# Spreading the mixer's loads over slots and sharing the second projection's weights between both halves, in a fused decoder layer

## The chip, the cores and the metric

One core of one Trainium2 chip runs the whole layer in one launch. The core has a matmul engine (TensorE, PE in the profile, with its weight loads listed as PEld), a vector engine (VectorE, DVE), a scalar engine (ScalarE, ACT), GpSimd (POOL), and SyncE (SP), whose queue issues almost all DMA transfers. SBUF is the on-chip memory, PSUM the banks that matmuls write, and DRAM lies off the core. The metric is the device time of one launch in microseconds, lower is better; shown are the median and the spread of several runs.

## The reference

One decoder layer on a sequence of 1024 tokens with a model width of 1024, in float32, with 256 memory tokens:

```python
h = rmsnorm(x, ln1)
ml_qk, ml_v, ml_o, ml_i, ml_f, fx_q, fx_k, fx_v, fx_f = split(h @ w_in)
ml_out = mlstm_chunkwise(...)            # 4 heads of width 128, normalised and gated
fx_out = forgetting_attention(...)       # 8 heads of width 64, causal
x = x + concatenate([ml_out, fx_out], -1) @ w_out          # 1024 x 1024
x = x + cross_attention(rmsnorm(x, ln_x), rmsnorm(mem, ln_mem), w_xq, w_xkv, w_xo)  # 4 heads of 256
u = relu(rmsnorm(x, ln2) @ w_ff1)        # 1024 x 4096
x = x + (u * u) @ w_ff2
out = rmsnorm(x, ln_f)
```

The change concerns the product with w_out, which joins the two groups of heads and adds the result to x, and the keys and values of the cross attention that are computed beside it.

## The kernel before

Activations lie with the model dimension on the 128 partitions, in 8 blocks (`KT`), and with the tokens in the free dimension, in two halves of 512 (`TH`, `hf`). A float32 factor is kept as two parts, hi (rounded to fp32r) and lo (the rest): `split` makes hi on ACT (line 130) and lo on DVE (line 131). A product is then three matmuls, lo by hi, hi by lo and hi by hi (`mm3`, lines 182 to 184), each of 512 columns. Weights come as raw tiles `wr`, in two buffers, and are cut into `wh` and `wl`.

**The mixer's result.** The four mLSTM heads and the attention's heads write their hi and lo parts to a DRAM tensor `mix[hf, part, partition, k]`. Its block index k runs over 8 blocks: 0 to 3 are the mLSTM heads, 4 the attention's heads 0 and 1, 5 heads 2 and 3, 6 heads 4 and 5, 7 heads 6 and 7. The product with w_out is done in two passes. The first uses k = 0 to 4 (`w_out_a`), runs while the attention is still going on, and writes x plus its partial sum to DRAM as `x1d`. The second uses k = 5 to 7 (`w_out_b`) and runs after the attention; it reads `x1d`, adds, and writes the sum back for later use.

**The attention's slots.** The attention runs as a list of slots (`slot`). In each, every engine gets a little of several steps at different stages: transposes of probabilities on PE (line 767, to PSUM bank `tp`), their cut into hi and lo, products with the values (line 786, to `ov`), scores of a later tile (lines 719 and 720, to `sc`), maxima on DVE, exponentials on ACT (line 741), scaling on POOL. `in_order` keeps the order of each engine as it is written, SP's among them in most slots; each engine works its queue in that order. One DMA of the next head's queries and keys is issued in each slot while there are any (`fx_step`, line 701, tensor `fqk`).

**The filler.** PE's time that the attention leaves in a slot is filled from a second list, `units`: 12 units that compute the cross attention's keys and values (`key_unit`, `value_unit`, results stored to `kxd` and `vxd`), and then 16 units of the first pass (`out_unit(hf, n)`, one for each half and output block n). A unit yields step by step to its slot. Its weights are cut by half tiles (line 965 on ACT, and DVE and POOL in turn for lo), and the raw load of the next ones is issued one slot after a cut (`raw_load`, line 952). `mix_in(0)` loads what half 0 needs of mix: two transfers of 1 MB into a tile `act` (line 850, k = 0 to 3, hi and lo) and two of 256 KB into a tile `z` (line 856, k = 4). It stands ten units into the list; `mix_in(1)` does the same for half 1 at `out_unit(0, 4)`. The residual tile of x comes with the unit that adds it (line 925, added at line 933). It and the results of the keys and values turn round in three buffers, `rotate("p", "a")`: two of tag p, one of tag a.

**The second pass.** After the slots, `mix_load` brings k = 5 to 7 of half 0, 768 KB for each part, and `out_proj` goes through the 8 output blocks of half 0 and then of half 1. A weight tile of 128x768 holds three k-blocks for two output blocks n; it is loaded and cut for each half anew, so eight times. `full_sink` adds `x1d`, stores the sum, splits it into `h2` for the cross attention, and has POOL add its squares to an accumulator (`acc`, DVE's tiles r_e among the squares). `row_second(hf, acc)` makes the normalising factors of one half: `rsqrt_sums` sums the squares with four small matmuls and takes the power on POOL, `to_row` turns them into a row by a transpose and a round trip through DRAM. It runs for half 0 at n = 2 of half 1, and for half 1 after the cross attention's first head of the first half. The cross attention follows, then the MLP.

```python
units += [out_unit(hf, n) for hf in range(2) for n in range(KT)]
...
fx_step()
part = next(parts, None)
...
todo_ = late[:]        # work that an earlier slot put off to this one
```

Of the kernel before, what the change touches and what calls it, by code (L numbers as in the profile page):

```python
# [17 lines left out]
P = 128  # L18
T = 1024
# [25 lines left out]
def hybrid_layer(ctx: ExitStack, tc: tile.TileContext, a: dict, out: bass.AP):  # L45
# [750 lines left out]
        v.tensor_tensor(out=om[hf][rng], in0=ov[0:FXD], in1=t[0:FXD], op=ALU.add)  # L796

    def fx_store(hd, hf):
        hi, lo = w2("y", dt=F32R), om[hf].bitcast(F32R)
        split(hi, lo, om[hf])  # L800

        def store():
            load(mix[hf, 0, :, MLH + hd // 2], hi.bitcast(F32))
            load(mix[hf, 1, :, MLH + hd // 2], lo.bitcast(F32))

        late.append(store)
# [37 lines left out]

    x1d = dram.tile([2, P, KT, TH], F32, name="x1d")

    def mix_load(k0, k1, hf):
        t = act().rearrange("p (e k) c -> p e k c", e=2)
        for p_ in range(2):
            load(t[:, p_, : k1 - k0].bitcast(F32), mix[hf, p_, :, k0:k1])  # L850
        return [(t[:, 0, k], t[:, 1, k]) for k in range(k1 - k0)]

    def mix_tile(k, hf):
        t = z4()[:, :T].bitcast(F32R).rearrange("p (e c) -> p e c", e=2)
        for p_ in range(2):
            load(t[:, p_].bitcast(F32), mix[hf, p_, :, k])
        return t[:, 0], t[:, 1]

    def out_proj(w_src, src, hf, sink):

        kn = len(src)
        per = w_src.shape[2] // (kn * P)
        for n in range(KT):
            if n % per == 0:
                w = both(weights(w_src[n // per], kn * per * P), lambda t: t.rearrange("p (k c) -> p k c", k=kn))
            at_ = n % per * P
            ps = mm()
            for k in range(kn):
                mm3(ps, both(w, lambda t: t[:, k, at_ : at_ + P]), src[k], k == 0, k == kn - 1)
            sink(n, hf, ps)  # L870


    late = []

    def void(_):
        return None

    def key_unit(n):
        def run(ws):
            w = both(ws[0], lambda t: t.rearrange("p (k c) -> p k c", k=KT))  # L880
            ps = mm()
            for k in range(KT):
# [12 lines left out]

        return [a["w_xk"][n]], run

    def value_unit(hd):
        def run(ws):
            ws = [both(w, lambda t: t.rearrange("p (k c) -> p k c", k=4)) for w in ws]  # L900
            for t in range(2):
                ps = mm()[:, :NM]
                for k in range(KT):
                    x = (hm[:, 0, k, t * P : (t + 1) * P], hm[:, 1, k, t * P : (t + 1) * P])
                    mm3(ps, x, both(ws[k // 4], lambda z: z[:, k % 4]), k == 0, k == KT - 1)
                    yield 1.5, k == KT - 1, lambda: sink(t, ps)

        def sink(t, ps):
            o = rotate("p", "a").bitcast(F32R).rearrange("p (e c) -> p e c", e=2)
# [5 lines left out]
    mixes = {}  # L915

    def mix_in(hf):
        mixes[hf] = mix_load(0, MLH, hf) + [mix_tile(k, hf) for k in range(MLH, MLH + KX)]

    def out_unit(hf, n):  # L920
        def run(ws):
            if n == 4 and hf == 0:
                mix_in(1)
            x = rotate("p", "a")
            load(x, a["x"][:, n, hf * TH : hf * TH + TH])
# [75 lines left out]
    def slot(values, until):  # L1001
        with in_order((*COMPUTE, mybir.EngineType.SP) if values or until else COMPUTE):
# [83 lines left out]
    while late:  # L1086
        late.extend(filter(None, [late.pop(0)()]))
    banks[:] = ["mm", "tp", "m2", "tp"]
    mix_fx = [mix_load(MLH + KX, KT, 0)]
    h2 = []  # L1090
    mix_done = []
    for hf in range(2):
        hi, lo = act(), act()
        acc = w2("b")

        def full_sink(n, hf, ps):
            t = rotate("p", "d", "e")
            with tc.issue_after(last_raw[0].ins):
                load(t, x1d[hf, :, n])
            v.tensor_tensor(out=t, in0=ps, in1=t, op=ALU.add)  # L1100
            done = load(x1d[hf, :, n], t)
            if hf == 0 and n == 1:
                with tc.issue_after(done.ins):
                    mix_fx.append(mix_load(MLH + KX, KT, 1))
            split(hi[:, n], lo[:, n], t, vec[:, VEC["ln_x"] + n :][:, 0:1])
            square_sum(acc, t, n == 0, add=g)
            if hf == 1 and n == KT - 3:
                mix_done.append(done)
            if hf and n == 2:
                row_second(0, acc0)  # L1110

        def row_second(hf, acc):
            c = rcol[:, 4 * hf : 4 * hf + 4]
            rsqrt_sums(acc, c, 4)
            at = slice(hf * TH, hf * TH + TH)
            to_row(row[:, at], c, 4, rowd[2:3, at])

        out_proj(a["w_out_b"], mix_fx[hf], hf, full_sink)
        h2.append((hi, lo))
        acc0 = acc  # L1120


    def cross_head(hd, hf, oh, ol):
# [174 lines left out]
    for hf in range(2):  # L1298
        oh, ol = act(), act()
        for hd in range(XH):  # L1300
# [5 lines left out]
            for _ in steps:  # L1306
                pass
            if hd == hf == 0:
                row_second(1, acc0)
        os_.append((oh, ol))  # L1310
    for n in range(2, KT):
        first_half(n)
# [362 lines left out]
```

## Time and profile before

| | |
|---|---|
| runs | 1532.7, 1533.2, 1538.22 us; median 1533.2 |
| profiled execution | 1537.44 us, of which the span of all engines' work is 1535.7 |
| mean granted clock of PE | 0.996 of full speed |
| busy | PE 1504.1, PEld 1260.2, DVE 1102.0, ACT 731.7, POOL 505.4 us |
| DMA | 303.53 MB moved, 198 GB/s over the span |
| attention with filler, up to the second pass | ends at about 610 us |
| second pass | about 610 to 656 us |

How to read the views that follow. In the timeline a row has the start in us, the duration, the engine, the line of the kernel, the operation with what it writes and reads (buffer numbers left out), and in brackets how long the engine had been idle before it and what ended that. "SPq" is SP's queue issuing a transfer, so its row gives when the transfer was handed over, not when the data came. The view of waits has for each waiting group and its releaser the sum, the number and the longest of the waits. The table of stretches has for each stretch of the span its length, then the busy time and the number of instructions of PE, PEld, DVE, ACT and POOL, the granted clock, the mean busy share of the DMA engines, and GB/s.

### The profile page before, as it was taken

The page shows a single profiled execution, that of the slowest core. Times are in us where ns is not written, and L with a number is a line of the kernel's source. Part 1 is how long each engine was busy: PE and PEld are TensorE (multiplying, and loading weights), DVE is VectorE, ACT ScalarE, POOL GpSimd, SP SyncE. Part 2 cuts the span into 40 slices and gives each one's busy share as a digit, 9 for nine tenths or more (in the row PEclk, how much of TensorE's full clock was granted, in tenths as well). Part 3 has the DMA queues.
Part 4 walks back from the last instruction along what each step waited for, and adds up shares of the span by engine and source line. Part 5 has one row for each costly group of instructions (what it writes and reads, how often), then busy time and mean ns, then how long its engine had stood idle before and what let it go on. Part 6 is the DMA issues. An engine that isn't in the chain of part 4 may idle for free. (4 is left out here: it accounts for less than half of the span.)

```text
span 1535.7 us, 21948 instructions
## 1 busy us (share of the span) xinstructions
PE 1504.1 (98%) x7665; PEld 1260.2 (82%) x7665; DVE 1102.0 (72%) x1747; ACT 731.7 (48%) x1365; POOL 505.4 (33%) x543
## 2 busy tenths in 40 slices
PE   8999999999999999999999999999999999999997
PEld 8878888889998878788888877787787888888887
DVE  7656676764787776944557889888887567887665
ACT  7324343334686665644444457666665621121224
POOL 1002030413364442521110023554454365563322
PEclk9999999999999999999999999999999999999999
DMA  6422223435889786963344428777667777776623
GB/s 221 124 76 76 96 104 117 134 128 155 245 243 262 228 262 205 349 211 118 124 131 162 167 90 296 245 250 243 227 246 273 303 288 270 275 271 238 246 96 110
DMA packets 121530, 303.53 MB, mean 198 GB/s; under 512 B 13502, under 2 KB 28152, under 8 KB 113996
## 3 DMA queue, kind: packets, MB, share of 16 engines
q1 hardware_dynamic: 121420, 302.13, 58.2%
q8 instruction: 60, 0.98, 0.3%
q14 instruction: 50, 0.41, 0.1%
HBM read 202.22 MB, written 99.86 MB: 197 GB/s over the span
## 5 line engine op out<-in xcount | busy, mean ns | idle before, releaser
L182 PE MATMUL tp<-act,wl 128*128 128x512 f32 (+1 forms) x448 | 176.2, 393 | 1.8 <-DMA act<-mix 0.8
L183 PE MATMUL tp<-act,wh 128*128 128x512 f32 (+1 forms) x448 | 175.4, 391 | 0.0
L184 PE MATMUL tp<-act,wh 128*128 128x512 f32 (+1 forms) x448 | 175.0, 392 | 0.0
L131 DVE TENSOR_TENSOR wl<-wr,wh 128x1024 fp32r<-128x1024 f32 (+2 forms) x99 | 129.7, 1310 | 20.8 <-ACT wh L130 19.9
L130 ACT ACTIVATE wh<-wr 128x1024 fp32r<-128x1024 f32 (+2 forms) x99 | 98.9, 1000 | 84.0 <-PE tp L184 36.5
L182 PE MATMUL mm<-act,wl 128*128 128x512 f32 (+1 forms) x336 | 129.8, 386 | 0.9 <-DVE r_c L514 0.9
L183 PE MATMUL mm<-act,wh 128*128 128x512 f32 (+1 forms) x336 | 129.2, 385 | 0.0
L184 PE MATMUL mm<-act,wh 128*128 128x512 f32 (+1 forms) x336 | 128.9, 383 | 0.0
L182 PE MATMUL m<-act,wl 128*128 128x512 f32 (+1 forms) x312 | 119.7, 384 | 3.1 <-DVE wl L131 2.1
L184 PE MATMUL m<-act,wh 128*128 128x512 f32 (+1 forms) x312 | 119.7, 384 | 0.0
L183 PE MATMUL m<-act,wh 128*128 128x512 f32 (+1 forms) x312 | 119.3, 382 | 0.0
L182 PEld LDWEIGHTS tp<-act,wl 128*128 128x128 f32 x448 | 84.2, 188 | 21.7 <-ACT row L1368 1.2
L184 PEld LDWEIGHTS tp<-act,wh 128*128 128x128 f32 x448 | 84.2, 188 | 19.2
L183 PEld LDWEIGHTS tp<-act,wh 128*128 128x128 f32 x448 | 84.2, 188 | 18.9
L182 PE MATMUL sc<-act,wl 128*128 128x512 f32 (+1 forms) x248 | 97.0, 391 | 0.9 <-DVE wl L131 0.8
L183 PE MATMUL sc<-act,wh 128*128 128x512 f32 (+1 forms) x248 | 96.7, 390 | 0.0
L184 PE MATMUL sc<-act,wh 128*128 128x512 f32 (+1 forms) x248 | 96.7, 390 | 0.0
L130 ACT ACTIVATE wh<-z 128x1024 fp32r<-128x1024 f32 (+1 forms) x54 | 55.5, 1027 | 82.6 <-POOL z L1439 60.9
L1439 POOL TENSOR_TENSOR z<-wr 128x256 f32<-128x256 f32 x56 | 50.4, 921 | 133.7 <-DMA wr<-w_ff2q 126.3
L131 DVE TENSOR_TENSOR wl<-z,wh 128x1024 fp32r<-128x1024 f32 (+1 forms) x54 | 74.8, 1385 | 9.8 <-ACT wh L130 9.7
L130 ACT ACTIVATE w<-wr 128x768 fp32r<-128x768 f32 (+2 forms) x31 | 25.5, 824 | 105.0 <-PE tp L182 32.8
L182 PEld LDWEIGHTS mm<-act,wl 128*128 128x128 f32 x336 | 63.4, 189 | 13.8 <-DVE r_c L514 1.2
(683 smaller groups left out, 4254.8 us busy)
## 6 DMA issues: line engine op xcount, KB each, us to landing
act<-right SPq DMA_DIRECT2D x49, 1024.0 KB
right<-w SPq DMA_DIRECT2D x56, 256.0 KB
wr<-w_ff2q SPq DMA_DIRECT2D x28, 512.0 KB
right<-r_d SPq DMA_DIRECT2D x49, 256.0 KB
right<-r_e SPq DMA_DIRECT2D x49, 256.0 KB
act<-fqk SPq DMA_DIRECT2D x48, 256.0 KB
wr<-w_in SPq DMA_DIRECT2D x20, 512.0 KB
wr<-w_ff SPq DMA_DIRECT2D x20, 512.0 KB
```

The costliest lines, as they stand in the source:

```text
L130: s.activation(hi, src, AF.Copy)
L131: return v.tensor_tensor(out=lo, in0=src, in1=hi.bitcast(F32), op=ALU.subtract)
L182: nc.tensor.matmul(ps, w[1], x[0], start=first, stop=False, skip_group_check=more)
L183: nc.tensor.matmul(ps, w[0], x[1], start=False, stop=False, skip_group_check=more)
L184: nc.tensor.matmul(ps, w[0], x[0], start=False, stop=last, skip_group_check=more)
L1439: g.tensor_tensor(out=o, in0=x, in1=y, op=op)
```

## The change

**Loads of mix in pieces.** `mix_in(hf)` only allocates its tiles, and puts ten copies of 256 KB (one for each k and part) on a list `pieces`. `mix_step`, called once in each slot behind `fx_step`, issues the first of them. `mix_in(0)` stands one unit earlier than before. What is left of the list when a half's first unit starts is issued there at once. SP's queue from the first mix load to the first weights of the first pass, before (raw weight buffers are `wr`, "x2" means two such rows):

```order
L952 DMA wr_5096<-w_xk 128x1024
L701 DMA act_3178<-fqk 64x1024
L850 DMA act_5122<-mix 128x2048 x2
L856 DMA z_886_5125<-mix 128x512 x2
L701 DMA act_3178<-fqk 64x1024
L829 DMA w_896_5159<-fvd 128x1024
L701 DMA act_3178<-fqk 64x1024
L892 DMA kxd<-r_p_5120 256x1x256
L952 DMA wr_5182<-w_out_a 128x640
```

and the same place of the changed kernel, from the second piece on (a first one stands two rows ahead):

```order
L919 DMA act_5021<-mix 128x512
L874 DMA kxd<-r_b_5017 256x1x256
L960 DMA wr_5100<-w_xk 128x1024
L701 DMA act_3178<-fqk 64x1024
L919 DMA act_5021<-mix 128x512
L701 DMA act_3178<-fqk 64x1024
L919 DMA act_5021<-mix 128x512
L834 DMA w_896_5159<-fvd 128x1024
L701 DMA act_3178<-fqk 64x1024
L919 DMA act_5021<-mix 128x512
L874 DMA kxd<-r_p_5125 256x1x256
L960 DMA wr_5183<-w_out_a 128x640
```

Two pieces stand ahead of the last w_xk, three between it and the first w_out_a, and five behind that.

**Residual tiles one unit ahead.** `x_in` loads the residual tile of the next unit, not of the unit that runs, and the tiles of units turn round in five buffers, `ROOM = ("p", "b", "p", "b", "a")`, not three. SP's queue where half 1's mix loads begin, before and after:

```order
L952 DMA wr_5755<-w_out_a 128x640
L850 DMA act_5801<-mix 128x2048 x2
L856 DMA z_1046_5804<-mix 128x512 x2
L925 DMA r_p_5807<-x 128x512
L701 DMA act_3178<-fqk 64x1024
L934 DMA x1d<-r_a_5699 128x512
L701 DMA act_3178<-fqk 64x1024
L952 DMA wr_5876<-w_out_a 128x640
```

Now, from the same load of w_out_a on:

```order
L960 DMA wr_5763<-w_out_a 128x640
L923 DMA r_b_5811<-x 128x512
L701 DMA act_3178<-fqk 64x1024
L919 DMA act_5809<-mix 128x512
L942 DMA x1d<-r_a_5614 128x512
L701 DMA act_3178<-fqk 64x1024
L919 DMA act_5809<-mix 128x512
L960 DMA wr_5882<-w_out_a 128x640
L701 DMA act_3178<-fqk 64x1024
L919 DMA act_5809<-mix 128x512
L923 DMA r_p_5905<-x 128x512
```

The residual tile r_b_5811 is that of the following unit, and the mix pieces stand behind it, one for each slot.

**The last two heads' results stay on chip.** `fx_store` puts the hi and lo parts of heads 6 and 7 into a tile of tag w4 for each half, not into mix. `mix_fx_in`, at the start of head 7's values, puts eight pieces (k = 5 and 6 of both halves) on the list, into one tile `act`. So `mix_load`, `mix_tile` and `out_proj` go.

**The second pass in chunks of four.** For output blocks 0 to 3 and then 4 to 7, two weight tiles are loaded and cut, and used for half 0 and then for half 1: four loads and cuts, not eight. Factors of half 0 are summed after block 6 of half 1, those of half 1 where they were, and one `to_row` then writes the row for both. PE's queue at the start of the second pass, before (tp, m and mm are PSUM banks, ov that of the attention's values):

```order
L786 MATMUL ov_6593<-r_d_6713,w_1173_6297 128x256
L182 MATMUL tp_6792<-act_6763,wl_6772 128x512
L786 MATMUL ov_6593<-w_1269_6724,w_1173_6297 128x256 x2
L182 MATMUL m_1271_6732<-act_5801,wl_6616 128x512
L183 MATMUL m_1271_6732<-act_5801,wh_6615 128x512
L184 MATMUL m_1271_6732<-act_5801,wh_6615 128x512
L182 MATMUL m_1271_6732<-z_1046_5804,wl_6616 128x512
```

and now, with w_1256 the kept result of heads 6 and 7 of half 0:

```order
L786 MATMUL ov_6612<-r_d_6734,w_1174_6311 128x256
L182 MATMUL tp_6813<-act_6528,wl_6787 128x512
L183 MATMUL tp_6813<-act_6528,wh_6786 128x512
L184 MATMUL tp_6813<-act_6528,wh_6786 128x512
L182 MATMUL tp_6813<-act_6528,wl_6787 128x512
L183 MATMUL tp_6813<-act_6528,wh_6786 128x512
L184 MATMUL tp_6813<-act_6528,wh_6786 128x512
L182 MATMUL tp_6813<-w_1256_6669,wl_6787 128x512
L183 MATMUL tp_6813<-w_1256_6669,wh_6786 128x512
```

The second pass's first block stands whole ahead of the attention's last products, which followed its first matmul before. The sums of half 0 (`row_second(0)`) now stand among the first matmuls of the cross attention's queries.

The diff, cut to its core:

```diff
     def fx_store(hd, hf):
+        if hd == FXH - 1:
+            t = w4(dt=F32R)
+            mix_fx[hf].append((t[:, :TH], t[:, TH:]))
+            split(*mix_fx[hf][-1], om[hf])
+            return
...
+            if hd == FXH - 1:
+                mix_fx_in()
...
+    ROOM = ("p", "b", "p", "b", "a")
...
-            t = rotate("p", "a").rearrange("p (e c) -> p e c", e=2)
+            t = rotate(*ROOM).rearrange("p (e c) -> p e c", e=2)
...
     def mix_in(hf):
-        mixes[hf] = mix_load(0, MLH, hf) + [mix_tile(k, hf) for k in range(MLH, MLH + KX)]
+        t = act().rearrange("p (e k) c -> p e k c", e=2)
+        mixes[hf] = [(t[:, 0, k], t[:, 1, k]) for k in range(MLH)]
...
+        pieces.extend((mixes[hf][k][p_], mix[hf, p_, :, k]) for k in range(MLH + KX) for p_ in range(2))
...
+    def mix_step():
+        if pieces:
+            dst, src = pieces.pop(0)
+            load(dst.bitcast(F32), src)
...
     def out_unit(hf, n):
         def run(ws):
+            while n == 0 and pieces:
+                mix_step()
             if n == 4 and hf == 0:
                 mix_in(1)
-            x = rotate("p", "a")
-            load(x, a["x"][:, n, hf * TH : hf * TH + TH])
+            if hf == 0 or n + 1 < KT:
+                x_in(hf + (n + 1) // KT, (n + 1) % KT)
+            x = xs.pop((hf, n))
...
-            if u == len(units) - 2 * KT - 2:
+            if u == len(units) - 2 * KT - 3:
                 mix_in(0)
+            if u == len(units) - 2 * KT - 1:
+                x_in(0, 0)
...
             fx_step()
+            mix_step()
...
+    for n0 in (0, 4):
+        ws = [weights(a["w_out_b"][n0 // 2 + i], 6 * P) for i in range(2)]
+        for hf in range(2):
...
+            for n in range(n0, n0 + 4):
...
+                full_sink(n, hf, ps)
+                if hf and n == 6:
+                    row_second(0)
```

More of the change, by code (lines that the diff above doesn't have):

```diff
@@ L845, in hybrid_layer @@
     x1d = dram.tile([2, P, KT, TH], F32, name="x1d")
[L847 to L870, printed above, removed]
     late = []
+    ROOM = ("p", "b", "p", "b", "a")
     def void(_):
@@ L908, in sink @@
         def sink(t, ps):
-            o = rotate("p", "a").bitcast(F32R).rearrange("p (e c) -> p e c", e=2)
+            o = rotate(*ROOM).bitcast(F32R).rearrange("p (e c) -> p e c", e=2)
             split(o[:, 0], o[:, 1], ps, rcol_m[:, t : t + 1])
@@ L1088, in hybrid_layer @@
     banks[:] = ["mm", "tp", "m2", "tp"]
-    mix_fx = [mix_load(MLH + KX, KT, 0)]
-    h2 = []
+    h2 = [(act(), act())]
+    x1_accs = [w2("b"), w2("b")]
     mix_done = []
[L1092 to L1120, printed above, removed]
@@ new lines, in full_sink, with row_second @@
+    def full_sink(n, hf, ps):
+        hi, lo = h2[hf]
+        t = rotate("p", "d", "e")
+        with tc.issue_after(last_raw[0].ins):
+            load(t, x1d[hf, :, n])
+        v.tensor_tensor(out=t, in0=ps, in1=t, op=ALU.add)
+        done = load(x1d[hf, :, n], t)
+        split(hi[:, n], lo[:, n], t, vec[:, VEC["ln_x"] + n :][:, 0:1])
+        square_sum(x1_accs[hf], t, n == 0, add=g)
+        if hf == 1 and n == KT - 3:
+            mix_done.append(done)
+    def row_second(hf):
+        rsqrt_sums(x1_accs[hf], rcol[:, 4 * hf : 4 * hf + 4], 4)
+        if hf:
+            to_row(row, rcol, 8, rowd[2:3])
@@ new lines, in hybrid_layer @@
+    for n0 in (0, 4):
+        ws = [weights(a["w_out_b"][n0 // 2 + i], 6 * P) for i in range(2)]
+        for hf in range(2):
+            if len(h2) <= hf:
+                h2.append((act(), act()))
+            for n in range(n0, n0 + 4):
+                w = both(ws[n // 2 % 2], lambda t: t.rearrange("p (k c) -> p k c", k=3)[:, :, n % 2 * P : n % 2 * P + P])
+                ps = mm()
+                for k in range(3):
+                    mm3(ps, both(w, lambda t: t[:, k]), mix_fx[hf][k], k == 0, k == 2)
+                full_sink(n, hf, ps)
+                if hf and n == 6:
+                    row_second(0)
@@ L1308, in hybrid_layer @@
             if hd == hf == 0:
-                row_second(1, acc0)
+                row_second(1)
         os_.append((oh, ol))
```

13 lines of the change are left out of this document (12 added, 1 removed).

## The prediction

> **What bounds the kernel now.** I read the page first, then the waits of the matmul engine, then the timeline around its longest waits, then a table by stretches.
>
> ```profile
> span 1535.7 us, 21948 instructions
> PE 1504.1 (98%) x7665; PEld 1260.2 (82%) x7665; DVE 1102.0 (72%) x1747; ACT 731.7 (48%) x1365; POOL 505.4 (33%) x543
> ```
>
> The matmul engine (PE) is busy for 98% of the span. Nearly every microsecond of the kernel is a matmul that the change keeps, so it can only win the time in which PE stands still or runs slowly. The stages that the change touches run from about 475 to 660 us. PE's waits of over half a microsecond there, from the view of waits:
>
> ```profile
> PE sc L719 <- ACT act L741: 4.6, 3, 3.2
> ...
> PE tp L767 <- DVE r_e L131: 1.1, 2, 0.9
> PE m L182 <- DVE r_e L1100: 1.0, 1, 1.0
> ...
> PE tp L182 <- DMA act<-mix: 0.8, 1, 0.8
> ```
>
> The columns are the sum, the number and the longest. The largest is a single wait of 3.2 us for the exponentials on ACT. The timeline tells what ACT had been doing:
>
> ```profile
> 498.70 0.47 ACT L965 ACTIVATE wh<-wr 128x320 fp32r<-128x320 f32 x1 [5.16 <-DMA wr<-w_out_a]
> ...
> 500.17 0.80 PE L719 MATMUL sc<-act 128*128 128x512 f32 x1 [3.23 <-ACT act L741]
> ...
> 504.60 0.63 PE L182 MATMUL mm<-act,wl 128*128 128x512 f32 x1
> 505.03 0.63 PE L183 MATMUL mm<-act,wh 128*128 128x512 f32 x1
> ...
> 506.22 0.39 PE L183 MATMUL mm<-act,wh 128*128 128x512 f32 x1
> 506.45 0.40 PE L184 MATMUL mm<-act,wh 128*128 128x512 f32 x1
> ```
>
> ACT works in program order. It idled 5.16 us at the head of its queue for the first weights of the first output projection, with the exponentials behind it; PE could cover 5.16 - 3.23 = 1.93 us of that. Then comes a second loss: from 500.17 to about 506 us a matmul of the same shape starts every 0.43 us (504.60 to 505.03) instead of every 0.23 us (506.22 to 506.45). The table of stretches has the cause, and how full the DMA engines are:
>
> ```profile
> 470.00:476.00 6.00, 6.00 (x50) 5.82 (x49) 4.26 (x15) 4.15 (x13) 3.55 (x7) 1.00 0.38 121
> ...
> 500.00:505.00 5.00, 4.83 (x15) 4.19 (x16) 3.88 (x11) 3.54 (x13) 2.49 (x6) 0.50 0.69 235
> ```
>
> After the five engines stand the granted clock (0.50 in the second row), the busy share of the DMA engines and GB/s. Half the clock over 5.9 us costs 5.9 x (0.43 - 0.23) / 0.43 = 2.7 us. The wait and its aftermath cost 3.2 + 2.7 = 5.9 us together.
>
> [...]
>
> **Spread mix loads.** Why were the weights late? The DMA queue (SP):
>
> ```profile
> 479.00 0.38 SPq L952 DMA_DIRECT2D wr<-w_xk  x1
> ...
> 479.94 1.06 SPq L850 DMA_DIRECT2D act<-mix  x2
> 481.04 1.33 SPq L856 DMA_DIRECT2D z<-mix  x2
> ...
> 487.37 0.34 SPq L952 DMA_DIRECT2D wr<-w_out_a  x1
> ```
>
> The first of the two raw-weight buffers got w_out_a at 487.37, and ACT could read it at 498.70. Since 479.00 these stood in the queue, by the shapes in the rows of SP's order shown with the change (one piece of fqk is 256 KB, and so on): w_xk 512 KB, fqk 256, mix 2560, fqk 256, fvd 512, fqk 256, kxd 256, and w_out_a itself 320, in all 4928 KB or 5.05 MB. They took 498.70 - 479.00 = 19.7 us, 256 GB/s with all delays in. The change puts two of its ten pieces of 256 KB ahead of w_xk, where the DMA engines were 38% busy (470 to 476), three between it and w_out_a, five behind. Left in the queue are 4928 - 2560 + 768 = 3136 KB or 3.21 MB, at 256 GB/s 12.5 us: w_out_a lands at 491.5 us, or 2.0 us later (0.52 MB) if the two early pieces still fill the queue, 493.5. ACT asks for it at 498.70 - 5.16 = 493.54. So I take this wait as gone, and the half clock with it: 5.9 us. Bounds: nothing is won if the stretch is full however the pieces are ordered; 5.9 is all there is. What is late next is the second w_out_a, with eight pieces ahead of it and wanted 3 us earlier than now; ACT may wait a microsecond for it, which PE's cover of 1.93 us hides.
>
> **The second half's mix loads and the early residual tiles.** Now another burst comes with its first out unit of the second four:
>
> ```profile
> 533.86 0.85 SPq L925 DMA_DIRECT2D r_p<-x  x1
> ...
> 545.11 0.69 DVE L933 TENSOR_TENSOR r_p<-mm,r_p 128x512 f32<-128x512 f32 x1 [4.45 <-DMA r_p<-x]
> ...
> 546.66 0.66 PE L767 MATMUL tp<-ident,act 128*128 128x128 f32 x4 [0.87 <-DVE r_e L131]
> ...
> 557.77 0.47 ACT L965 ACTIVATE wh<-wr 128x320 fp32r<-128x320 f32 x1 [1.91 <-DMA wr<-w_out_a]
> ...
> 534.00:546.00 12.00, 11.62 (x62) 9.26 (x61) 6.34 (x22) 6.60 (x19) 5.18 (x10) 1.00 1.02 352
> ...
> 550.00:560.00 10.00, 10.00 (x52) 8.04 (x51) 6.23 (x15) 6.57 (x19) 3.51 (x5) 1.00 1.04 266
> ```
>
> The residual tile was issued behind the burst and came 11.3 us later; DVE waited 4.45 us for it with a transposed block behind, and PE 0.87 us. Issued one unit earlier, into five rotating buffers instead of three, and with no burst ahead, it is on time: 0.9 us won. But the ten pieces now run on to about 560 us, and from 550 to 560 the DMA engines are full without them (1.04), while ACT already waits 1.91 us for weights there, just what PE covers. Half of the pieces (1.3 MB) in that stretch are 5 us of queue at 266 GB/s; the older burst's remainder is gone in exchange. Between nothing and 5 us of weights being later I take 0.3 us lost on PE, near nothing, because now as before the same bytes pass between 531 and 562 us. SP issues 28 small copies where it issued twelve, at 0.3 to 0.4 us each in the rows above and below; SP is not on PE's path, so that costs nothing as long as no piece waits for its buffer.
>
> **Results kept on chip.** The second projection now starts on loads that come late:
>
> ```profile
> 605.40 0.32 SPq L850 DMA_DIRECT2D act<-mix  x1
> ...
> 606.29 0.38 SPq L850 DMA_DIRECT2D act<-mix  x1
> ...
> 611.38 0.47 PE L182 MATMUL tp<-act,wl 128*128 128x512 f32 x1 [0.77 <-DMA act<-mix]
> ...
> 613.83 0.19 PEld L183 LDWEIGHTS mm<-act,wh 128*128 128x128 f32 x1 [0.33 <-DMA act<-mix]
> ```
>
> With heads 6 and 7 kept in SBUF, and heads 2 to 5 loaded in pieces from the start of head 7 on, both waits go: 0.77 + 0.33 = 1.1 us. Four stores of 256 KB and as much loading go as well; they lay beside matmuls.
>
> **The second projection in chunks.**
>
> ```profile
> L131 DVE TENSOR_TENSOR wl<-wr,wh 128x768 fp32r<-128x768 f32 x8 | 9.8, 1227 | 2.2 <-ACT wh L130 2.2
> ...
> L130 ACT ACTIVATE wh<-wr 128x768 fp32r<-128x768 f32 x8 | 6.6, 842 | 2.3 <-PE m L184 1.5 <-PE mm L184 0.8
> ...
> 639.64 0.50 PE L182 MATMUL m<-act,wl 128*128 128x512 f32 x1 [0.26 <-DVE wl L131]
> ...
> 655.11 0.50 PE L182 MATMUL m<-act,wl 128*128 128x512 f32 x1 [0.98 <-DVE r_e L1100]
> ...
> 612.00:660.00 48.00, 46.77 (x204) 37.10 (x203) 41.28 (x49) 30.20 (x46) 22.59 (x15) 1.00 0.99 348
> ```
>
> Each block of weights is used for both halves, so four of eight loads and cuts go: 4 x 1.227 = 4.9 us of DVE and 4 x 0.842 = 3.4 us of ACT, beside matmuls. DVE is busy 41.28 of 48 us here, and both PE waits of the stage (0.26 and 0.98) are for DVE; 36.4 of 48 leaves it slack. The order at the end changes too: the row sums of half 0 stand in PE's queue among the first query matmuls, and POOL takes their power after six more additions. Between nothing and 1.2 us I take 0.8. One transpose and one small round trip through DRAM fewer (the row of norm factors is written once, later): nothing, its readers come after the cross attention.
>
> **The sum.** 5.9 + 0.9 - 0.3 + 1.1 + 0.8 = 8.4 us from the profiled execution's 1537.44 (span 1535.7): 1529.0. The runs shown are 1532.7, 1533.2 and 1538.22, so the profiled one is 4.2 above the median; its half clock (2.7) is the only part of that the trace names. If the median run lacks it, it becomes 1533.2 - (8.4 - 2.7) = 1527.5. I forecast **1528 us**.
>
> **Rivals.**
> 1. *More goes than PE's own waits show.* The ACT waits for weights and the small PE waits that follow them go too. All PE waits of these stages on both bounds (0.9 + 1.1 + 1.2 + 3.2 = 6.4), and the ACT wait of 1.91 as well, give 1533.2 - 6.4 - 1.9 = 1525, or some 1524 with the last unnamed gaps. For: each late DMA delays a queue with the next slot's work. Against: most of that lies under PE's cover.
> 2. *It doesn't do what it says.* The stretch is full either way, and the first weights are as late as now. For: the same bytes pass in the same stretch, and from the burst to the weights the DMA engines are nearly all full already:
>
> ```profile
> 476.00:480.00 4.00, 3.55 (x29) 3.31 (x28) 2.88 (x7) 3.95 (x12) 1.79 (x2) 1.00 0.86 262
> ...
> 488.00:492.00 4.00, 4.00 (x34) 3.88 (x33) 3.71 (x8) 3.51 (x11) 0.70 (x2) 1.00 1.05 293
> ```
>
> Against: a third of the bytes now ahead of the weights would stand behind them. Only the second projection wins: 1533.2 - 1.9 = 1531.3 for the median run, 1535.5 for the profiled one; about 1533.
> 3. *Slower: the small pieces choke the stretch around 560.* Every slot puts a piece ahead of a weight load; in 550 to 560 us the DMA engines are at 1.04 already, and ACT's wait of 1.91 us uses up PE's cover, so each further microsecond is PE's. It decides when the pieces add more than about 2 us to each weight load. With the full 5 us of queue at three loads in a row, and the slow clock twice, 1528 + 3 x 3.1 + 2 x 2.7 = 1543. Against: the second projection's stretch, all copies of 256 to 512 KB, moves 348 GB/s, the most of the rows here beside the burst's own 352, so small copies as such aren't slow.
>
> [...] No run yet shows the pieces themselves.
>
> **How the numbers follow.** The forecast (1526 to 1533) gets 0.52, the first rival 0.23, the second 0.16, the slower one 0.09. The range that leaves out two in ten reaches from 1523 into the second rival, to 1536. A measurement of this kernel can tell about 0.5% (7.7 us) from no change: faster means below 1525.5, slower above 1540.9. Faster gets the first rival's larger part and a little of the forecast, 0.27; slower 0.08; the rest is the same, 0.65.
>
> **What would show it.** Right: no ACT wait of over 2 us for w_out_a, the clock at 1.00 from 475 to 660, no wait for mix ahead of the second projection, and no PE wait over 1 us at its end. Wrong: new ACT waits for weights between 550 and 570, DMA share over 1 with lower GB/s while pieces run, or PE waiting where the row sums of half 0 stand. A gain far above 8.4 us would mean that stages after 700 us moved too; there the order of PE, ACT and DVE is the same up to where the cross attention ends.

## The result, and the profile after

The changed kernel takes 1525.32 us (median of 4, 1523.82 to 1526.68) against 1535.18 us before (median of 4, 1532.7 to 1538.22). The ratio is 0.9934, 95% interval 0.9921 to 0.9946: 0.66% or 10 us faster. The forecast was 1528 us and the range 1523 to 1536. The time lies in the range, but just below the 1526 to 1533 that went with the forecast, at the first rival's number, 1525, and past the 0.5% for which only a chance of 0.27 was given.

The profiled execution took 1525.33 us, so span against span the gain is 1535.7 - 1523.6 = 12.1 us (the one of before was 2.3 us above its median). The head of its page:

```profile
span 1523.6 us, 21919 instructions
PE 1499.0 (98%) x7664; PEld 1258.4 (83%) x7664; DVE 1098.5 (72%) x1743; ACT 727.6 (48%) x1360; POOL 507.1 (33%) x543
```

The PE waits of over half a microsecond from 475 to 660 us are all gone. What is left for the exponentials over the whole kernel stands in these two rows of the waits. The longest of the first is 0.5 us, as before the change, and the longest of the second lies at 433 us, ahead of the stages that changed:

```profile
PE sc L719 <- ACT w L741: 1.5, 4, 0.5
PE sc L719 <- ACT act L741: 1.4, 2, 1.0
```

ACT waits for a w_out_a only once in that stretch, for 0.7 us; the wait of 1.91 us near 557 us went too.

SP's queue and ACT at the old trouble spot, from the timeline:

```profile
485.35 0.54 SPq L960 DMA_DIRECT2D wr<-w_out_a  x1
...
494.06 0.47 ACT L973 ACTIVATE wh<-wr 128x320 fp32r<-128x320 f32 x1
```

ACT cuts the first w_out_a at 494.06 us without any idle time ahead (before: 5.16 us of it, until 498.70). The stretches that answer to those of before:

```profile
470.00:476.00 6.00, 6.00 (x48) 5.79 (x47) 4.60 (x15) 4.54 (x13) 3.07 (x6) 1.00 0.31 87
...
488.00:492.00 4.00, 4.00 (x36) 3.98 (x35) 3.68 (x7) 3.90 (x11) 1.21 (x2) 1.00 1.04 326
500.00:505.00 5.00, 5.00 (x32) 4.25 (x30) 3.63 (x12) 2.90 (x10) 2.47 (x5) 1.00 1.00 343
...
550.00:560.00 10.00, 10.00 (x55) 8.39 (x55) 7.44 (x24) 6.87 (x21) 4.38 (x8) 1.00 0.86 296
602.00:650.00 48.00, 48.00 (x213) 38.67 (x211) 37.11 (x48) 26.66 (x41) 22.03 (x15) 1.00 0.83 272
```

The clock is 1.00 from 500 to 505 us (0.50 before), PE is busy for all 48 us of the second pass (46.77 before), and DVE is busy 37.1 us there and not 41.3.

To compare kernels whose times differ by less than their spread, I use one more measure, worked out from the matmul rows of each trace and called the loss below: for each two neighbouring matmuls the time from start to start, less what their shape takes when nothing waits (231 ns for 512 columns, 175 for 384, 125 for 272, 117 for 256, 108 for 128 and fewer, the usual steps in these traces), summed over a stretch, in us. It holds waits and slow clock alike; some 0.2 us in 25 us are left where nothing waits. "Slow clock" is the length of the records with a granted clock of 0.5 between 480 and 640 us. Ratios are to the kernel before, run beside each. The loss is that of the profiled execution alone, whose time stands in its own column; where it lies far from the median, the loss doesn't describe the median run.

| kernel | median us | ratio (95%) | profiled us | loss 475-525 | 525-600 | 600-675 | 875-1000 | slow clock |
|---|---|---|---|---|---|---|---|---|
| before (profile above) | 1535.18 | | 1537.44 | 8.6 | 3.2 | 3.7 | 4.9 | 6.83 |
| changed | 1525.32 | 0.9934 (0.9921-0.9946) | 1525.33 | 2.4 | 1.1 | 0.9 | 3.4 | 0 |
| ctl_before | 1535.76 | 0.9999 (0.9988-1.0010) | 1533.45 | 7.5 | 2.8 | 3.7 | 3.9 | 3.41 |
| only_spread | 1532.13 | 0.9978 (0.9966-0.9991) | 1532.59 | 3.0 | 3.5 | 3.9 | 5.0 | 0 |
| only_residual | 1532.95 | 0.9980 (0.9971-0.9990) | 1534.02 | 7.1 | 1.6 | 4.1 | 3.9 | 3.41 |
| first_pass | 1529.03 | 0.9964 (0.9952-0.9976) | 1531.51 | 2.4 | 1.1 | 5.2 | 4.9 | 0 |
| only_chunks | 1540.50 | 1.0037 (1.0024-1.0050) | 1543.26 | 9.2 | 3.4 | 10.4 | 3.0 | 6.83 + 6.83 |
| only_onchip | 1533.86 | 0.9986 (0.9975-0.9997) | 1529.21 | 5.2 | 1.5 | 2.2 | 3.6 | 0 |
| second_pass | 1531.56 | 0.9981 (0.9971-0.9992) | 1531.69 | 9.2 | 1.1 | 0.6 | 3.2 | 6.83 |
| after_burst | 1529.97 | 0.9970 (0.9958-0.9982) | 1529.69 | 7.9 | 1.1 | 0.6 | 3.3 | 3.41 |
| burst_early | 1535.28 | 0.9998 (0.9987-1.0009) | 1534.91 | 7.1 | 1.7 | 3.9 | 4.2 | 3.41 |
| after_start10 | 1525.34 | 0.9926 (0.9915-0.9938) | 1525.07 | 3.4 | 1.1 | 1.6 | 2.8 | 0 |
| pieces_128 | 1526.91 | 0.9934 (0.9922-0.9946) | 1525.45 | 4.0 | 1.2 | 0.6 | 3.0 | 0 |
| pieces_512 | 1531.53 | 0.9966 (0.9953-0.9980) | 1533.64 | 11.1 | 1.3 | 0.6 | 3.3 | 6.83 |

Each profile is one execution, so a column can't be told to better than about a microsecond (the two of before differ by 1.1, 0.4, 0.1 and 1.0).

### The profile page after: what moved, and what is told of

Same layout as the page of the kernel before. It is cut to its first block, busy times and chain, and to the rows that moved or that the text cites. A ratio compares the mean times of both kernels' runs of the same rounds, so it can differ in the third digit from the quotient of the medians.

```text
span 1523.6 us, 21919 instructions
## 1 busy us (share of the span) xinstructions
PE 1499.0 (98%) x7664; PEld 1258.4 (83%) x7664; DVE 1098.5 (72%) x1743; ACT 727.6 (48%) x1360; POOL 507.1 (33%) x543
## 5 line engine op out<-in xcount | busy, mean ns | idle before, releaser
L182 PE MATMUL tp<-act,wl 128*128 128x512 f32 (+1 forms) x440 | 172.9, 393 | 1.2 <-ACT row L1381 0.7
L183 PE MATMUL tp<-act,wh 128*128 128x512 f32 (+1 forms) x440 | 172.2, 391 | 0.0
L184 PE MATMUL tp<-act,wh 128*128 128x512 f32 (+1 forms) x440 | 171.8, 391 | 0.0
L131 DVE TENSOR_TENSOR wl<-wr,wh 128x1024 fp32r<-128x1024 f32 (+2 forms) x95 | 124.4, 1309 | 23.9 <-ACT wh L130 23.4
L130 ACT ACTIVATE wh<-wr 128x1024 fp32r<-128x1024 f32 (+2 forms) x95 | 95.7, 1007 | 79.2 <-PE tp L184 34.2
L184 PE MATMUL mm<-act,wh 128*128 128x512 f32 (+1 forms) x332 | 127.3, 384 | 0.0
L183 PE MATMUL mm<-act,wh 128*128 128x512 f32 (+1 forms) x332 | 127.2, 383 | 0.0
L184 PE MATMUL m<-act,wh 128*128 128x512 f32 (+1 forms) x308 | 117.8, 382 | 0.0
L183 PE MATMUL m<-act,wh 128*128 128x512 f32 (+1 forms) x308 | 117.6, 382 | 0.0
```

What stands on the lines that cost most here:

```text
L130: s.activation(hi, src, AF.Copy)
L131: return v.tensor_tensor(out=lo, in0=src, in1=hi.bitcast(F32), op=ALU.subtract)
L182: nc.tensor.matmul(ps, w[1], x[0], start=first, stop=False, skip_group_check=more)
L183: nc.tensor.matmul(ps, w[0], x[1], start=False, stop=False, skip_group_check=more)
L184: nc.tensor.matmul(ps, w[0], x[0], start=False, stop=last, skip_group_check=more)
```

## The experiments

**ctl_before: the same kernel again.** No edit.

> The kernel before once more, for a second profile of the same program. If the slow stretch behind the 3.2 us wait belongs to the wait (theory: every PE wait of about 3 us here is followed by some 6 us at half clock), the profile shows again about 3.2 us of PE waiting for the exponentials near 497 us and then a granted clock near 0.5 from 500 to 505 us, and the time is 1535 to 1538 us. [...]

1535.76 us, and in the profiled execution (1533.45) the wait came back with a slow stretch, but one half as long. The stretches of its profile, cut at the clock's own steps:

```profile
495.46:498.87 3.41, 0.12 (x1) 0.12 (x2) 0.60 (x1) 1.59 (x6) 0.86 (x1) 1.00 1.01 343
498.87:502.28 3.41, 3.41 (x13) 3.03 (x14) 2.73 (x9) 2.43 (x8) 1.01 (x2) 0.50 0.63 196
502.28:505.69 3.41, 3.41 (x18) 2.87 (x17) 2.36 (x8) 2.08 (x8) 1.48 (x5) 1.00 0.41 129
```

and of the first profile of before, cut in the same way:

```profile
495.86:499.27 3.41, 1.07 (x8) 0.64 (x6) 0.00 (x0) 0.57 (x2) 0.00 (x0) 1.00 1.06 277
499.27:502.68 3.41, 2.52 (x10) 2.32 (x11) 2.66 (x8) 2.79 (x9) 0.87 (x1) 0.50 0.80 274
502.68:506.10 3.42, 3.42 (x10) 2.74 (x10) 2.41 (x6) 1.49 (x5) 2.34 (x5) 0.50 0.42 155
```

The first number behind the length is PE's busy time, the third from the end the clock. In ctl_before PE was busy for 0.12 of 3.41 us, then came one slow window in which it was busy throughout, then full clock. In the first profile it was busy for 1.07 of 3.41 us, then came a slow window with 2.52, and a second slow one. So in these two profiles the slow clock behind the wait had no fixed price: it came in windows of 3.41 us, one in ctl_before, where the wait ended just ahead of the slow window, and two in the first profile, where it reached 0.89 us into it. The last section has the busy shares of all runs together.

**only_spread, only_residual and first_pass: the first pass's two edits, each alone and both.** Mix loads in pieces:

```diff
-        mixes[hf] = mix_load(0, MLH, hf) + [mix_tile(k, hf) for k in range(MLH, MLH + KX)]
+        pieces.extend((mixes[hf][k][p_], mix[hf, p_, :, k]) for k in range(MLH + KX) for p_ in range(2))
...
+            mix_step()          # in each slot, behind fx_step()
```

Residual tiles:

```diff
-            x = rotate("p", "a")
-            load(x, a["x"][:, n, hf * TH : hf * TH + TH])
+            if hf == 0 or n + 1 < KT:
+                x_in(hf + (n + 1) // KT, (n + 1) % KT)      # the next unit's, ROOM of five
+            x = xs.pop((hf, n))
```

> The kernel before with the mix loads in ten pieces, one per slot and one unit earlier, and nothing else of the change. Theory (the order of the bytes ahead of the weights is what costs): ACT's wait of 5.16 us for the first weights of the first pass is gone, no PE wait over 1 us from 475 to 525 us, the burst behind which the residual tile stood is gone too so that most of the 0.87 us PE wait at 545 goes, the waits at 610, 640 and 655 us stay (2.0 us): about 7 us less than before, 1528. Rival (the early residual tiles are needed for it): 6 us less at most, the DVE wait for the residual tile stays over 3 us. Rival (the stretch is full either way): 1533 to 1535.

> The kernel before with residual tiles one unit ahead and five rotating buffers, mix loads in bursts as before. Theory (order of bytes): the 3.2 us PE wait near 497 us stays, the tile that is issued ahead of the second burst is on time and the 0.87 us wait at 545 us goes: 1 us less than before, 1534. Rival (the larger rotation also frees the key and value stores, so that SP's queue moves up): 2 to 4 us less.

> The kernel before with both edits on the first pass (mix loads in pieces, residual tiles one unit ahead in five buffers), and the second pass as before. The spread alone left DVE 4.8 us waiting for a residual tile near 553 us, the residual edit alone left the wait for the exponentials. Theory (the two need each other): PE loses about 2.5 us from 475 to 525 (8.0 before) and 1.1 from 525 to 600 (3.0 before), 3.7 from 600 to 675 as before; 7.4 us less than before, 1528. Rival (they only add up as they did alone, 4.5 to 5.6 and 1.2 to 2.7 with part of it counted twice): 5 us less, 1530 to 1531.

only_spread took 1532.13 us and not 1528. The wait near 497 us went as the theory said (loss from 475 to 525: 3.0). But the second half's trouble did not go; it moved to 551 to 555 us, as the timeline shows:

```profile
551.13 0.47 ACT L977 ACTIVATE wh<-wr 128x320 fp32r<-128x320 f32 x1 [2.65 <-DMA wr<-w_out_a]
...
552.70 0.50 PE L719 MATMUL sc<-act 128*128 128x512 f32 x1 [0.67 <-ACT act L741]
...
553.38 0.69 DVE L945 TENSOR_TENSOR r_p<-mm,r_p 128x512 f32<-128x512 f32 x1 [4.82 <-DMA r_p<-x]
...
555.13 0.33 PE L767 MATMUL tp<-ident,act 128*128 128x128 f32 x1 [1.00 <-DMA mix<-r_y]
```

DVE waits 4.82 us for a residual tile issued at 544.49, ACT 2.65 us for weights: close to what the third rival foresaw, though the longer wait is for a residual tile, and at the price of 0.67 + 1.00 us on PE and not of 15. only_residual did what was expected of it (1532.95; DVE waits for no residual tile there) and left the first wait (2.85 us). Both together bring the loss from 475 to 600 us from 11.8 to 3.5 and the time to 1529.03 us, 5.5 us less than before by the ratio, where the theory had 7.4. In the profiled execution the second pass that follows gave 1.5 us back (5.2 against 3.7), with this wait in it:

```profile
642.74 0.50 PE L182 MATMUL mm<-act,wl 128*128 128x512 f32 x1 [1.76 <-DVE wl L131]
```

That execution took 1531.51 us, the longest of five, so the median run need not have this wait. How much of the stretch 525 to 600 us belongs to the residual edit stays open: only_onchip and second_pass, which have the old bursts and the old residual loads, lost only 1.5 and 1.1 us there in their one profile.

**only_chunks, only_onchip and second_pass: the second pass's two edits.** Chunks alone keeps the loads of k = 5 to 7 from DRAM, both halves asked for at the start:

```diff
-    mix_fx = [mix_load(MLH + KX, KT, 0)]
+    mix_fx = [mix_load(MLH + KX, KT, hf) for hf in range(2)]
...
+    for n0 in (0, 4):           # two weight tiles, four blocks of half 0, then of half 1
```

On chip alone is the edit of `fx_store` and `mix_fx_in` with the old order of blocks; second_pass has both.

> The kernel before with the second pass in chunks of four blocks for both halves, all of its mix blocks still loaded from DRAM, both halves at the start. Theory: DVE has slack, so the waits of 0.26 and 0.98 us at the end of the pass go, but the start now waits for 3 MB and not 1.5 MB: half 1 is wanted only after four blocks, so the 0.77 + 0.33 us at 610 us stay and nothing more: 1 us less, 1534. Rival: the two weight tiles at the head of the queue and the double load hold up the first block by several us: 1537 to 1540.

> The kernel before with the last two heads' results kept and k = 5 and 6 loaded in pieces, output blocks in the old order with eight weight loads. Theory: the waits for mix at 610 us go (1.1 us), those for DVE at 640 and 655 us (0.3 to 0.8 and 1.0) stay: PE loses about 2.5 us from 600 to 675, 1534. Rival (the chunks do nothing of their own, all of the second pass's gain is the loads'): 0.9 us there, 1532.5.

> The kernel before with both edits on the second pass (last two heads' results kept, k = 5 and 6 loaded in pieces from head 7 on, chunks of four blocks for both halves), the first pass as before. Chunks alone lost 5.6 us waiting for half 1's blocks of mix. Theory (that wait was only because the blocks came in bulk at the start of the pass): PE loses 0.9 us from 600 to 675 as in the changed kernel, 3.7 before, so 2.8 us less, 1532.5. Rival (the waits of the start return while the first pass's bursts are there): 1534 to 1536.

Chunks alone is slower, 1540.50 us; the rival was right. The reason is in its timeline:

```profile
616.00 0.32 SPq L803 DMA_DIRECT2D mix<-r_y  x1
...
621.04 3.34 SPq L850 DMA_DIRECT2D act<-mix  x2
...
628.28 0.79 PE L182 MATMUL mm<-act,wl 128*128 128x512 f32 x1 [5.42 <-DMA act<-mix]
```

Half 1's blocks can be read only after the last heads' results have been stored (616.00), so they are issued at 621.04, and half 1 now comes after four blocks and not after eight: PE waits 5.42 us, and two windows at half clock follow. Kept on chip, the results need no store and no reload. only_onchip took 1533.86 us and left 2.2 us of loss, 1.20 us of it for DVE at the end; second_pass left 0.6 us and took 1531.56 us. So the chunks are worth about 1.5 us behind the kept results by these profiles (0.8 us by the two ratios, whose intervals overlap), and cost about 6.7 us (10.4 - 3.7) without them: the prediction priced the two edits one by one, but the chunks have no price without the kept results. The profiled execution of only_onchip, 1529.21 us, is the fastest of its twelve and has no slow clock, which its median run need not share.

**after_burst, burst_early and after_start10: spread, or early?** The changed kernel with the ten pieces at once, where the burst stood:

```diff
+        while pieces:
+            mix_step()          # in mix_in
...
-            if u == len(units) - 2 * KT - 3:
+            if u == len(units) - 2 * KT - 2:
```

The kernel before with its old burst one unit earlier (2 to 3 in that line, nothing else), and the changed kernel with spread pieces that start one unit later (3 to 2, nothing else).

> The changed kernel with its ten mix pieces issued all at once and one unit later, where the burst stood before; pieces of the same 256 KB, residual tiles early. Theory (it is the order ahead of the weights, not the size of the copies): ACT waits 4.5 to 5.5 us for the first weights again, PE about 3 us, then some us at half clock, loss from 475 to 525 again 7 to 9 us against 2.4: 1530 to 1532. Rival (early residual tiles and larger rotation do it): within 1.5 us of the changed kernel, 1525 to 1527. If small copies as such were slow, it would be over 1533.

> The kernel before with its mix bursts in the old form, half 0's one unit earlier (behind a load of w_xv at about 474 us, where the DMA engines were 38% busy), and nothing else of the change. Theory (who stands behind the burst waits): now it is w_xk, issued behind it and wanted at 484.8 us; 3.93 MB at 256 GB/s land at 489.6, ACT waits 4 to 5 us near 488 us, PE some 3, with the slow clock again, and the first w_out_a is in time: 1534 to 1536, as before. Rival (an earlier start alone cures it, since the same bytes then have 5 us more): PE loses under 3.5 us from 475 to 525 us: 1529 to 1531.

> The changed kernel with the first pieces one unit later, where the burst stood, so that no piece uses the stretch at 470 to 476 us in which the DMA engines were 31 to 38% busy; two pieces and not five stand ahead of the first weights, and three are issued at once when the first unit starts. Theory: weights are in time (0.5 MB ahead of them and not 1.3), no loss from 475 to 500; but the last pieces are now what the first unit waits for: 0.5 to 2 us more than the changed kernel, 1526 to 1527. Rival (the early start is the cure, not the spread): the wait near 497 us returns with 2 to 3 us and the slow clock, 1530.

after_burst lost the first edit's gain again, 1529.97 us. (SP took 6.4 us to issue the ten copies one after another, so its first w_out_a was handed over at 489.25, 1.9 us later than before; burst_early has the four transfers of before.)

```profile
498.84 0.47 ACT L975 ACTIVATE wh<-wr 128x320 fp32r<-128x320 f32 x1 [5.58 <-DMA wr<-w_out_a]
...
500.30 0.80 PE L719 MATMUL sc<-act 128*128 128x512 f32 x1 [3.65 <-ACT act L741]
```

burst_early is as slow as before, 1535.28 us; now it is the load behind the burst, w_xk, that is late, by the 5 us that were expected:

```profile
490.50 0.63 ACT L965 ACTIVATE wh<-wr 128x512 fp32r<-128x512 f32 x1 [5.01 <-DMA wr<-w_xk]
...
493.09 0.39 PE L719 MATMUL sc<-act 128*128 128x256 f32 x1 [2.85 <-ACT act L741]
```

after_start10 takes 1525.34 us, as the changed kernel does; there is no wait for w_out_a. So the spread is the cure, and the early start is not needed. That the wait moves to whichever load stands behind the burst is shown by the pair of before and burst_early.

**pieces_128 and pieces_512: the size of a piece.**

```diff
-        pieces.extend((mixes[hf][k][p_], mix[hf, p_, :, k]) for k in range(MLH + KX) for p_ in range(2))
+        pieces.extend((t[:, :, k], mix[hf, :, :, k].rearrange("e p c -> p e c")) for k in range(MLH))    # 512 KB; z as before
```

and for 128 KB each piece in two column halves, two of them in each slot.

> The changed kernel with the first pass's mix blocks in pieces of 128 KB, two in each slot: the same bytes in the same slots, rows of 1 KB and not 2 KB on each partition, and twice as many issues. Theory (size does not decide here, the order does): same as the changed kernel within 1 us, 1525. Rival (small copies choke the stretch): the bursts of 2.6 MB take some us longer, ACT waits over 2 us for weights or DVE for residual tiles near 550 us, 2 to 6 us more: 1527 to 1531.

> The changed kernel with the first pass's mix blocks k = 0 to 3 in pieces of 512 KB (hi and lo of one block in one transfer), so that four slots carry what eight did; the last two stay at 256 KB. Theory (order ahead of the weights decides, size does not): 3.5 MB instead of 3.1 MB stand ahead of the first weights, 1.6 us of queue more; ACT asks at about 494 us and gets them by then or waits under 1 us. PE loses 2.4 to 3 us from 475 to 525 and 1.1 to 1.5 from 525 to 600; 1525 to 1526.5. [...]

pieces_128 took 1526.91 us, 1.6 us more than the changed kernel and after_start10, though the intervals of the ratios (0.9934, and 0.9934 and 0.9926 for those two) overlap. Its profile shows a small price: ACT waits four times for w_out_a, 4.1 us in total, and PE waits for the last pieces of half 0:

```profile
504.96 0.47 PE L183 MATMUL mm<-z,wh 128*128 128x512 f32 x1 [1.39 <-DMA z<-mix]
```

That is nearly all of the 1.6 us by which its loss from 475 to 525 us exceeds the changed kernel's (4.0 against 2.4). pieces_512 was a miss: 1531.53 us. ACT waits twice:

```profile
489.59 0.63 ACT L974 ACTIVATE wh<-wr 128x512 fp32r<-128x512 f32 x1 [3.99 <-DMA wr<-w_xk]
...
502.75 0.47 ACT L974 ACTIVATE wh<-wr 128x320 fp32r<-128x320 f32 x1 [6.44 <-DMA wr<-w_out_a]
```

Part of it is the order: 1 MB of pieces stands ahead of w_xk and 1.25 MB between it and w_out_a, where the changed kernel has 0.5 and 0.75, and w_out_a can only be issued when w_xk has been cut. But the DMA engines also moved less while they were as busy. The stretches of pieces_512:

```profile
480.00:488.00 8.00, 7.18 (x50) 6.47 (x51) 6.41 (x20) 4.52 (x14) 4.83 (x8) 1.00 1.06 257
488.00:496.00 8.00, 6.15 (x47) 5.66 (x46) 4.98 (x11) 6.24 (x16) 1.95 (x2) 1.00 1.04 243
```

and of the changed kernel:

```profile
480.00:488.00 8.00, 7.33 (x51) 6.61 (x52) 6.27 (x20) 5.49 (x16) 5.59 (x9) 1.00 1.04 319
488.00:496.00 8.00, 8.00 (x63) 7.65 (x62) 7.36 (x16) 7.16 (x21) 2.86 (x5) 1.00 1.05 316
```

257 and 243 GB/s against 319 and 316, at a busy share of 1.04 to 1.06 in all four. Whether the transfer's form (hi and lo in one) or its neighbours make it slow is open. A larger transfer was not the better one in this stretch: the old bursts (338 and 287 GB/s in the same two windows of the kernel before) lost, the pieces of 512 KB moved least, and only the step from 256 to 128 KB (321 and 282 GB/s), with its small waits, went the other way.

## Why the prediction was right, and where it was not

**The first wait and its slow clock: 5.9 us forecast, 6.1 measured** (loss from 475 to 525: 8.6 to 2.4), and 5.4 by after_burst against the changed kernel. The mechanism held: the queue of bytes ahead of the weights. One reason in it wasn't needed: that two pieces use the empty stretch ahead (after_start10).

**The slow clock as chance.** The prediction took from three runs that the median execution may lack it, and went from 1529.0 to 1528 for that. No profiled run of the kernel before shows that term, its wait without the 2.7 us of half clock; only_onchip, with a wait of 2.53 us and no half clock, comes nearest. With more runs the median of before is 1535.1 to 1536.2 us, and the slow clock stood in six of the seven other kernels' profiles with a PE wait of 2.5 us or more between 475 and 525 us, for one window or two. The mean clock of every run agrees: the changed kernel's four and all of after_start10, pieces_128, first_pass and only_spread, whose profiles have no slow window between 480 and 640 us, are at 0.997 or 0.998; of 86 runs of the kernel before beside the experiments and in ctl_before 54 are at 0.994 to 0.996 and four at 0.998. So the step of 1 us for it was not sound, and the base of 1533.2 us was some 2 us low. The forecast came out 2.7 us above the measured time since two terms were too small and one was missing (below): from profile to profile the terms measured 6.1 + 2.1 + 1.2 + 1.6 + 1.5 = 12.5 us where the sum had 8.4 (the spans differ by 12.1). Against ctl_before's profile the same terms are 5.1 + 1.7 + 0.9 + 1.9 + 0.5 = 10.1, near the 9.9 us between the medians, so each size is good to about a microsecond. That 1528 came so close, and lies in its range, is partly luck: a gain some 4.7 us too small (5.2 from the base to the forecast, 9.9 measured) was set off in part by a base 2 us too low.

**The second half's loads and the residual tiles: 0.6 us forecast, 2.1 measured** (3.2 to 1.1). The term of 0.3 us for later weights at 550 to 560 us did not come, and the smaller waits around the 0.87 us one went too, which the sum had left out. That these two edits did it is not shown: second_pass, which has neither, also lost only 1.1 us there in its profile. only_spread shows that the fear was sound: without the early residual tiles the choke is there.

**Results kept on chip: 1.1 forecast, 1.2 measured** (600 to 625 us: 1.35 to 0.17). **Chunks: 0.8 forecast, 1.6 measured** (625 to 675: 2.30 to 0.72). The upper bound of 1.2 us was too low, since it counted only the two waits that the view names. And the step that priced the chunks by themselves, with DVE's slack alone, fails: only_chunks costs 5 us.

**After 675 us: nothing forecast, 1.5 us measured** (875 to 1000: 4.9 to 3.4; 0.5 from ctl_before's 3.9). The step "there the order of PE, ACT and DVE is the same up to where the cross attention ends" does not hold. By the traces, between 665 and 823 us DVE has another instruction in 36 places of its order and ACT in 34, in the same way in all eight kernels with an edit of the second pass. One such place on DVE, at the end of the cross attention, before:

```profile
819.67 0.69 DVE L131 TENSOR_TENSOR act<-ov,act 128x512 fp32r<-128x512 f32 x1 [0.29 <-ACT act L130]
820.28 0.68 DVE L1274 TENSOR_TENSOR r_y<-mm,r_y 128x512 f32<-128x512 f32 x1
```

and after:

```profile
808.17 0.69 DVE L1287 TENSOR_TENSOR r_y<-mm,r_y 128x512 f32<-128x512 f32 x1
...
811.30 0.69 DVE L131 TENSOR_TENSOR act<-ov,act 128x512 fp32r<-128x512 f32 x1
```

The new order gains nothing where it stands (from 660 to 875 us the loss is 1.9 us in all fourteen profiles), and behind it the order of DVE and ACT is the old one. The gain comes in the MLP. Before, from its timeline:

```profile
937.71 0.27 PE L245 MATMUL mm<-ident,gcol 128*8 128x128 f32 x1
938.05 1.22 DVE L131 TENSOR_TENSOR wl<-wr,wh 128x1024 fp32r<-128x1024 f32 x1
...
939.32 0.50 PE L182 MATMUL m<-act,wl 128*128 128x512 f32 x1 [1.34 <-DVE wl L131]
```

and after:

```profile
925.86 1.22 DVE L131 TENSOR_TENSOR wl<-wr,wh 128x1024 fp32r<-128x1024 f32 x1
...
926.89 0.28 PE L245 MATMUL mm<-ident,gcol 128*8 128x128 f32 x1
...
927.13 0.50 PE L182 MATMUL m<-act,wl 128*128 128x512 f32 x1
```

The same cut begins 0.34 us after that small matmul before and 1.03 us ahead of it after. In all eight profiles with an edit of the second pass the loss from 875 to 1000 us is 2.8 to 3.6 us, in all six without one 3.9 to 5.0. The wait of the row above is 1.34 us in three of these six, 0.45 to 0.70 in the other three, and in none of the eight. So an edit of the second pass, perhaps through the new order in the cross attention that comes with it, leaves PE and DVE in another step to each other; which of the two does it, no run here separates.

**The rivals.** The first, that more goes than PE's named waits, is what happened in the stages that it names, and it had 0.23; that its 1525 is the measured time is luck, since it took 8.3 us off a base 2 us too low and knew nothing of the stretch after 675 us. The second (full either way) is refuted by only_spread and after_burst. The third, the choke near 560 us, came up in only_spread, at a small price, and not in the changed kernel.

## What to carry to other kernels

Look at a late load by what was issued ahead of it on its queue; spread a large transfer that nobody needs yet between the small ones that somebody does, since here moving it as a whole only made another load late. Price edits together where one supplies what the other needs sooner. And count what follows a PE wait: here each of the nine of 2.8 us or more behind the first matmul was followed by half clock. In the stretch from 475 to 525 us that cost another 1.7 to 1.8 us (one window) or 2.3 to 3.1 us (two): the loss there less the waits and less the 2.4 us that the changed kernel loses too.

## What the runs showed of the hardware

Between 480 and 640 us the slow clock came in steps of 3.413 us (every record of it there is 3413 or 6827 ns long). Cut into windows of that length in step with the records, the traces give PE's busy share of the last window at full clock: 0.00 (after_burst), 0.04 (ctl_before), 0.10 and 0.11 (only_chunks), 0.20 (only_residual), 0.27 (second_pass), 0.31 (before), 0.37 (burst_early) and 0.39 (pieces_512) were followed by half clock; between 25 us and the last few microseconds of the kernel no window at full clock with 0.49 or above was. One 0.49 is first_pass's, at 641 us; the other is only_onchip's, whose 2.53 us wait fell across two windows:

```profile
494.26:497.68 3.42, 2.65 (x19) 2.13 (x17) 0.39 (x1) 0.00 (x0) 0.63 (x2) 1.00 1.05 327
497.68:501.09 3.41, 1.65 (x11) 1.56 (x12) 1.82 (x5) 3.11 (x10) 0.86 (x1) 1.00 0.85 315
501.09:504.50 3.41, 3.41 (x19) 2.83 (x18) 3.38 (x11) 2.56 (x10) 2.53 (x5) 1.00 0.55 180
```

But the share alone doesn't decide. At the end of every profile the clock is halved too, and the window ahead of that was busy between 0.29 and 0.54 of its time, as in first_pass with 1.85 of 3.42 us:

```profile
1518.18:1521.60 3.42, 1.85 (x14) 1.47 (x12) 1.53 (x5) 1.63 (x4) 1.44 (x2) 1.00 0.62 212
1521.60:1525.01 3.41, 1.22 (x4) 0.93 (x4) 1.93 (x6) 0.00 (x0) 0.00 (x0) 0.50 0.01 2
```

So up to 0.39 all windows at full clock were followed by half clock, above 0.54 none, and in between both happened; what decides there is open. Between 480 and 640 us the clock went back to full after a slow window that was busy 0.94 or more, and not after 0.28 (pieces_512), 0.32 and 0.80 (only_chunks), 0.48 (second_pass) and 0.74 (before). Half clock also came behind windows that were not idle throughout (0.39 busy in pieces_512), and behind waits of 2.85 us, shorter than a window (only_residual, burst_early).
